# A decoder layer's down projection computed as seven block products instead of eight

## The chip, the cores and the metric

The kernel runs on one core of a Trainium2 chip. The metric is device time in microseconds (us) for one execution. Five engines run their own instruction lists in order and wait for each other by semaphores: TensorE (PE in the rows, its weight loads PEld), VectorE (DVE), ScalarE (ACT), GpSimd (POOL) and SyncE (SP), which here issues every DMA.

## The reference

One layer of a hybrid decoder over 1024 tokens of width 1024, in float32. Attention and a recurrent mixer come first; only the feed-forward block at the end bears on the change:

```python
D_MODEL = SEQ = 1024;  D_FF = 2816
...
xn2 = rms_norm(x, norm2_g)
ffn = (jax.nn.silu(xn2 @ w_gate) * (xn2 @ w_up)) @ w_down
return x + ffn
```

The last product, (1024 x 2816) times (2816 x 1024), is the down projection. Its left factor, silu(gate) times up, is called the hidden activation below.

## The kernel before

**Who sets the order.** The program is written as streams, generators that yield instructions. A planner (`Flow`) holds an estimate of every instruction's time and emits next, from the stream that can go first, so the order on each engine is fixed when the program is built. `Wait` and `Mark` in a stream steer the planner alone; on the chip the engines wait for the data and buffers that an instruction touches. `flow.add(rank, stream)` gives a stream its place among others that are ready together.

**Operands.** PE multiplies in a reduced float32. To keep accuracy each factor is split in two: ACT copies it into a rounded high part (`oph`), another engine subtracts that from the source to get the low part (`opl`), in `split`, called by `operand` (line 1587). A product then takes three matmuls: high times high, high times low, low times high (`passes`). `operand` works on blocks of 128 x 512 and keeps NOPS = 5 pairs of buffers, so operand n can be prepared once operand n - 5 has been read by PE for the last time. Loaded blocks lie in NFRAW = 6 buffers, `fraw`, filled by `fetch_ff` (line 1568) through SP. Every matmul here is 128 x 128 times 128 x 512.

**Gate and up stage.** `ffproj` (line 1659) goes through 22 feature blocks p of 128. From p = NCL = 2 on it already uses a seven-product scheme over the two halves of the tokens and of the width: products P1, P6, P2, P7, P5, P4, P3, twelve matmuls each, 84 for a block p. POOL prepares the low parts of three operands and two weight sums (`sw`), DVE the other sums and low parts. `gates` and `hidden` (lines 1685 and 1712) add the products up from PSUM into `uu` and `up`, apply silu on ACT, multiply, and store the hidden activation, feature by token, to DRAM (`h_d`).

**Down projection.** `down` (line 1762) loops over two token halves th, 22 feature blocks f, two halves of the output columns and four token blocks, with three matmuls each: 2 x 22 x 2 x 4 x 3 = 1056. For a pair (th, f) three operands are loaded and prepared, one of `h_d` and two of `w_down`, all low parts on DVE. Eight PSUM banks accumulate over f. `finals` (line 1787) adds each bank to the residual `acc[j]` and stores it.

Below, a *turn* means the work on one pair of operands in the changed down projection: twelve matmuls.

## Time and profile before

| what | before |
|---|---|
| median of three runs | 1492.36 us (1490.73 to 1492.68) |
| the profiled execution | 1501.24 us, of it span of the trace 1499.4 us |
| granted clock of TensorE over the span, full speed = 1 | 0.973 |
| PE busy over the span | 1426.3 us (95%) |
| DVE / ACT / POOL busy | 801.1 / 714.3 / 539.8 us |
| HBM read / written | 130.26 / 37.75 MB |

How to read it: "busy" is the time in which an engine has an instruction under way. A matmul's row lasts 389 ns because its end is modelled at the end of the pipeline; the next one starts about 0.227 us after it. A "window" row gives the busy time of each engine in a stretch of the span. "Idle before <- releaser" names the instruction that ended the wait.

### The profile page before, as it was taken

To read this page: it belongs to the slowest core of one execution; us is meant where nothing else is said; L and a number is where in the kernel's file an instruction comes from. 1 tells how busy PE (TensorE), PEld (TensorE's weight loads), DVE (VectorE), ACT (ScalarE), POOL (GpSimd) and SP (SyncE) were. 2 spreads that over 40 slices of the span, in tenths; PEclk is the share of its full clock that TensorE was granted. 3 is DMA by queue.
4 is the path that set the end of the run, shared out by engine and by line. 5 is a ranking of instruction groups with operands and counts; after the bars stand their busy time and mean duration, and the time that the engine had idled before them with its cause. 6 is when DMAs were issued, how large, how long until landed. Compare 5 with 4: busy or idle time off the path is not lost. (4 is left out here: it accounts for less than half of the span.)

```text
span 1499.4 us, 24765 instructions
## 1 busy us (share of the span) xinstructions
PE 1426.3 (95%) x8710; PEld 1155.9 (77%) x8710; DVE 801.1 (53%) x1799; ACT 714.3 (48%) x1768; POOL 539.8 (36%) x564
## 2 busy tenths in 40 slices
PE   8999989999999986799999899999999999999999
PEld 5677767777778865688888678888888888888887
DVE  5456677657656337666776734443444434334334
ACT  5434556576676775555855433333333333333332
POOL 4432344255645451422454733444444440000000
PEclk8999999999999988799999999999999999999999
DMA  5343222323323344998521222222222224445443
GB/s 192 108 120 75 65 82 78 99 76 110 115 87 103 105 150 125 276 248 224 151 63 50 84 78 85 85 83 79 75 79 80 85 77 134 148 148 197 148 148 126
DMA packets 199789, 173.83 MB, mean 116 GB/s; under 512 B 39025, under 2 KB 150897, under 8 KB 199666
## 3 DMA queue, kind: packets, MB, share of 16 engines
q1 hardware_dynamic: 199666, 172.26, 38.3%
q8 instruction: 69, 1.13, 0.3%
q14 instruction: 54, 0.44, 0.1%
HBM read 130.26 MB, written 37.75 MB: 112 GB/s over the span
## 5 line engine op out<-in xcount | busy, mean ns | idle before, releaser
L235 ACT ACTIVATE oph<-fraw 128x512 fp32r<-128x512 f32 x208 | 126.3, 627 | 228.7 <-PE chain L235 97.9
L235 POOL TENSOR_TENSOR opl<-fraw,oph 128x512 fp32r<-128x512 f32 x76 | 99.6, 1315 | 220.6 <-PE bank L235 71.3
L235 DVE TENSOR_TENSOR opl<-fraw,oph 128x512 fp32r<-128x512 f32 x132 | 87.5, 689 | 143.6 <-ACT oph L235 143.6
L235 ACT ACTIVATE oph<-sw 128x512 fp32r<-128x512 f32 x80 | 50.6, 632 | 179.4 <-DVE sw L235 71.5
L235 POOL TENSOR_TENSOR inlo<-inraw,inhi 128x512 fp32r<-128x512 f32 x62 | 82.2, 1326 | 84.8 <-ACT inhi L235 70.6
L235 PE MATMUL bank<-opl,oph 128*128 128x512 f32 x176 | 68.5, 389 | 0.0
L235 PE MATMUL bank<-oph 128*128 128x512 f32 x176 | 68.5, 389 | 0.0
L235 PE MATMUL bank<-oph,opl 128*128 128x512 f32 x176 | 68.5, 389 | 0.0
L235 DVE TENSOR_TENSOR opl<-sw,oph 128x512 fp32r<-128x512 f32 x80 | 56.0, 699 | 21.0 <-ACT oph L235 17.2
L235 DVE TENSOR_TENSOR uu<-bank,uu 128x512 f32<-128x512 f32 x20 | 13.8, 692 | 81.7 <-PE bank L235 81.7
L235 DVE SCALAR_TENSOR_TENSOR S<-chain,ec,Sp 64x64 f32<-64x64 f32 x112 | 31.6, 282 | 43.1 <-PE chain L235 38.5
L235 ACT ACTIVATE Ub<-chain 64x64 f32<-64x64 f32 x128 | 28.2, 220 | 54.6 <-DVE VS L235 52.4
L235 POOL TENSOR_TENSOR sw<-fraw 128x512 f32<-128x512 f32 x40 | 52.0, 1299 | 0.0
L235 ACT ACTIVATE Y<-chain 64x64 f32<-64x64 f32 x128 | 26.9, 212 | 51.1 <-DVE S L235 45.8
L235 ACT ACTIVATE inhi<-inraw 128x512 fp32r<-128x512 f32 x62 | 38.7, 624 | 16.7 <-DMA inraw<-in_w_in_dram 6.7
L235 DVE COPY Rb<-chain 64x64 f32<-64x64 f32 x128 | 28.9, 226 | 27.9 <-PE chain L235 25.4
L235 POOL TENSOR_TENSOR up<-up,sg 128x512 f32<-128x512 f32 x20 | 32.3, 1617 | 30.1 <-POOL sw L235 16.1
L235 ACT ACTIVATE sb<-sb,mx 128x256 f32<-128x256 f32 (+3 forms) x64 | 36.2, 567 | 14.4 <-DVE mx L235 14.3
L235 PEld LDWEIGHTS bank<-oph,opl 128*128 128x128 f32 x176 | 33.0, 188 | 6.9
L235 PEld LDWEIGHTS bank<-oph 128*128 128x128 f32 x176 | 33.0, 188 | 6.8
L235 PEld LDWEIGHTS bank<-opl,oph 128*128 128x128 f32 x176 | 33.0, 188 | 6.8
L235 POOL TENSOR_TENSOR rsf<-smf,nhalf 128x8 f32<-128x8 f32 x16 | 26.6, 1662 | 31.6 <-DVE smf L235 31.3
(494 smaller groups left out, 4228.6 us busy)
## 6 DMA issues: line engine op xcount, KB each, us to landing
fraw<-in_w_down_dram SPq DMA_DIRECT2D x88, 256.0 KB, 2.8
inraw<-in_w_in_dram SPq DMA_DIRECT2D x62, 256.0 KB, 2.9
fraw<-in_w_gate_dram SPq DMA_DIRECT2D x48, 256.0 KB, 3.7
fraw<-in_w_up_dram SPq DMA_DIRECT2D x48, 256.0 KB, 3.0
fraw<-h_d SPq DMA_DIRECT2D x44, 256.0 KB, 2.9
h_d<-up SPq DMA_DIRECT2D x42, 256.0 KB, 2.1
rkv_d<-stage SPq DMA_DIRECT2D x24, 256.0 KB, 2.9
xt<-in_x_dram SPq DMA_DIRECT2D x8, 512.0 KB, 7.3
```

The source lines that it names most:

```text
L235: op.fn(*op.a, **op.k)
```

## The change

The eight block products of the down projection become seven over pairs of feature blocks (2m, 2m+1), in Winograd's form of Strassen's scheme. The hidden activation, as A11, A12, A21, A22 by token half and by feature block of the pair, gives four sums S1 to S4; w_down, as B11 to B22 by feature block and by column half, gives four sums T1 to T4. The seven products are P1 = A11 B11, P2 = A12 B21, P3 = S4 B22, P4 = A22 T4, P5 = S1 T1, P6 = S2 T2, P7 = S3 T3, each over m = 0 to 10: 77 turns of twelve matmuls.

- `weight_sums` (new): while the gate and up stage runs, POOL forms T1 to T4 from w_down in the buffers of `acc0` and `acc1`, whose residual is spilled to DRAM and loaded again afterwards; SP stores the sums to `t_d`.
- `halves` (new, in `hidden`): DVE forms S1 to S4 (for a pair of blocks p six operations where there were two); SP stores them to `s_d`. A21 is no longer stored.
- `fetch_ff`: the first three turns are loaded through `fraw`, the others through four new buffers `raw2` in the space of B22, which PE reads up to its last product of the gate and up stage.
- `prepare_ff`: the low part of a turn's first operand (a, of the hidden activation) stays on DVE, that of its second (b, of the weights) goes to POOL.
- `finals`: P1 goes to `acc` and, by ACT, to `U2`; P6 is added to `U2` by DVE, and POOL then adds `U2` to three parts of `acc` for each of four token blocks. P4 accumulates on P7's banks and P3 on P5's once DVE has read them (`dtaken`).

```diff
-    blocks2 = [(th, f, j, "down") for th in range(2) for f in range(NFF) for j in range(3)]
...
+    turns2 = [(x, m) for x in ("P1", "P6", "P7", "P4", "P5", "P3", "P2") for m in range(NP)]
+    factors = {"P1": ("A11", "B11"), "P2": ("A12", "B21"), "P3": ("S4", "B22"), "P4": ("A22", "T4"),
+               "P5": ("S1", "T1"), "P6": ("S2", "T2"), "P7": ("S3", "T3")}
+    NEARLY = NFRAW // 2
...
+        yield Wait(("P3", NFF - 1))
+        for n, (x, m) in enumerate(turns2[NEARLY:]):
+            if n >= 4:
+                yield Wait(("rawfree2", n - 4))
+            raw = T(PX, [128, 2, 4, 128], F32, "raw2", tag="x1", bufs=4)
+            for j in range(2):
+                src, mark = factor(factors[x][j], m)
+                yield Wait(*([mark] if mark else []))
+                yield SP.dma_start(raw[:, j].rearrange("p k t -> p (k t)"), src)
...
+    def weight_sums():
...
+        yield Wait(*[("x2", i) for i in range(4, 8)])
+        for m in range(NP):
+            ws = [T(pacc, [128, 2, HB], F32, f"ws{i}", tag=f"acc{i}") for i in range(2)]
+            for i in range(2):
+                f = 2 * m + i
+                yield SP.dma_start(ws[i].rearrange("p q t -> p (q t)"), w_down[f * 128:(f + 1) * 128, :])
+            (b11, b12), (b21, b22) = [[w[:, q, :] for q in range(2)] for w in ws]
+            for j, o_, a_, b_ in ((1, b11, b12, b11), (3, b12, b22, b12), (2, b22, b22, b11), (4, b21, b21, b22)):
+                yield POOL.tensor_tensor(out=o_, in0=a_, in1=b_, op=ALU.subtract)
+                yield SP.dma_start(t_d[j - 1][m * 128:(m + 1) * 128], o_)
...
+        for n, (x, m) in enumerate(turns2):
+            for j in range(2):
+                key = (x, m, j, "down")
+                yield Wait(("raw", key))
+                yield from operand(key, fraws[key], POOL if j else DVE)
...
+    flow.add(23, weight_sums())
...
+            if p % 2 == 0:
+                held[0] = T(PG, [128, HB], F32, "first", bufs=4)
+                yield DVE.tensor_tensor(out=held[0], in0=c22, in1=c12, op=ALU.mult)
+                held[1] = T(PG, [128, HB], F32, "first", bufs=4)
+                yield DVE.tensor_tensor(out=held[1], in0=c21, in1=held[0], op=ALU.subtract)
+                yield SP.dma_start(s_d[2][both], held[1])
...
+            else:
+                yield DVE.tensor_tensor(out=c22, in0=c22, in1=c12, op=ALU.mult)
+                yield SP.dma_start(h_d[rows, HB:S], c22)
...
+                yield DVE.tensor_tensor(out=s2, in0=c22, in1=held[1], op=ALU.subtract)
+                yield SP.dma_start(s_d[1][both], s2)
...
+    after = {"P4": "P7", "P3": "P5"}
...
+        for x, m in turns2:
...
+            for t in range(4):
+                if m == 0 and x in after:
+                    yield Wait(("dtaken", after[x], t))
+                    downs[x, t] = downs[after[x], t]
...
+                for n, (a_, b_) in enumerate(passes(ah, al, bh, bl)):
+                    yield PE.matmul(out=downs[x, t][0], lhsT=a_[:, t, :], rhs=b_.rearrange("p k t -> p (k t)"),
...
+                if x == "P1":
+                    yield ACT.activation(U2[:, t, :], ps, AF.Copy)
+                yield DVE.tensor_tensor(out=out_, in0=ps, in1=out_, op=ALU.add)
...
+                if x == "P6":
+                    for i, c in ((t, hi), (4 + t, lo), (4 + t, hi)):
+                        yield POOL.tensor_tensor(out=acc[i][:, c], in0=acc[i][:, c], in1=U2[:, t, :], op=ALU.add)
```

The order on PE, DVE, ACT, POOL and SP is the same in both programs up to the feed-forward block. Three places in it, with the rows as the built programs have them (tiles, output before input; the number behind a tile tells buffers apart).

SP in the gate and up stage, before: one block p (`up` holds hidden activations, `fraw` the loaded weights).

```order
L235 DMA fraw<-in_w_up_dram 128x4x128
L235 DMA h_d<-up_11329 128x512
L235 DMA h_d<-up_11310 128x512
L235 DMA fraw<-in_w_up_dram 128x4x128
L235 DMA fraw<-in_w_gate_dram 128x4x128 x2
```

SP at the same place, after (`ws` weight sums, `first` held S sums).

```order
L235 DMA t_d<-ws_10435 128x512
L235 DMA fraw<-in_w_up_dram 128x4x128
L235 DMA t_d<-ws_10435 128x512
L235 DMA h_d<-up_10519 128x512
L235 DMA t_d<-ws_10436 128x512
L235 DMA s_d<-first 128x512
L235 DMA fraw<-in_w_up_dram 128x4x128
L235 DMA fraw<-in_w_gate_dram 128x4x128 x2
L235 DMA t_d<-ws_10436 128x512
L235 DMA ws_10607<-in_w_down_dram 128x1024
L235 DMA ws_10608<-in_w_down_dram 128x1024
```

The stores of weight sums, which wait for POOL, and the stores of S sums, which wait for DVE, now stand ahead of weight loads that were there alone.

POOL in the gate and up stage, before: one block p.

```order
L235 TENSOR_TENSOR up_11776<-up_11776,sg_11717 128x512
L235 TENSOR_TENSOR opl<-fraw,oph 128x512 x2
L235 TENSOR_TENSOR sw_11872<-fraw 128x512
L235 TENSOR_TENSOR opl<-fraw,oph 128x512
L235 TENSOR_TENSOR sw_11912<-fraw 128x512
L235 TENSOR_TENSOR up_11925<-up_11925,sg_11866 128x512
```

POOL at the same place, after.

```order
L235 TENSOR_TENSOR opl<-fraw,oph 128x512
L235 TENSOR_TENSOR sw_10627<-fraw 128x512
L235 TENSOR_TENSOR ws_10607<-ws_10607 128x512
L235 TENSOR_TENSOR opl<-fraw,oph 128x512
L235 TENSOR_TENSOR sw_10670<-fraw 128x512
L235 TENSOR_TENSOR ws_10607<-ws_10608,ws_10607 128x512
L235 TENSOR_TENSOR up_10683<-up_10683,sg_10621 128x512
L235 TENSOR_TENSOR ws_10608<-ws_10608,ws_10607 128x512
L235 TENSOR_TENSOR opl<-fraw,oph 128x512
L235 TENSOR_TENSOR ws_10608<-ws_10608 128x512
```

Four subtractions on `ws` now stand between the low parts, the `sw` sums and the product `up`.

POOL at the end of the gate and up stage, before; it has nothing behind these rows.

```order
L235 TENSOR_TENSOR sw_12806<-fraw 128x512
L235 TENSOR_TENSOR up_12819<-up_12819,sg_12760 128x512
L235 TENSOR_TENSOR opl<-fraw,oph 128x512
L235 TENSOR_TENSOR up_12969<-up_12969,sg_12909 128x512
L1856 UNCONDITIONAL_BRANCH
```

POOL after, where the down projection goes from P6 to P7 (`raw` is raw2, `U` is U2; the first row is the b operand of P7's turn 0).

```order
L235 TENSOR_TENSOR opl<-raw_13658,oph 128x512
L235 TENSOR_TENSOR acc_11600<-acc_11600,U_13477 128x512
L235 TENSOR_TENSOR acc_6839<-acc_6839,U_13477 128x512
L235 TENSOR_TENSOR opl<-raw_13681,oph 128x512
L235 TENSOR_TENSOR acc_6839<-acc_6839,U_13477 128x512
L235 TENSOR_TENSOR opl<-raw_13704,oph 128x512
L235 TENSOR_TENSOR acc_11604<-acc_11604,U_13477 128x512
L235 TENSOR_TENSOR opl<-raw_13727,oph 128x512
L235 TENSOR_TENSOR acc_6840<-acc_6840,U_13477 128x512 x2
L235 TENSOR_TENSOR opl<-raw_13751,oph 128x512
```

The low part of every turn now goes through POOL, and between those of P7's turns 0 to 9 stand twelve additions to `acc`.

## Rows read from the trace of the kernel before

**Rows 1.** The page: span; busy time of each engine, share of span, count
```profile
span 1499.4 us, 24765 instructions
...
PE 1426.3 (95%) x8710; PEld 1155.9 (77%) x8710; DVE 801.1 (53%) x1799; ACT 714.3 (48%) x1768; POOL 539.8 (36%) x564
```

**Rows 2.** Busy by stage: window, length, each engine with count, PEclk, DMA share, GB/s
```profile
1064.94:1084.23 19.29, 19.29 (x86) 15.76 (x85) 7.80 (x13) 6.14 (x10) 8.00 (x6) 1.00 0.27 82
1260.00:1490.00 230.00, 229.99 (x1015) 190.15 (x1014) 88.28 (x135) 75.06 (x126) 0.00 (x0) 1.00 0.44 148
```

**Rows 3.** Timeline, first and last matmul of the down projection, and last sum
```profile
1255.88 0.39 PE L235 MATMUL mm<-oph 128*128 128x512 f32 x1
...
1495.38 0.39 PE L235 MATMUL chain<-oph,opl 128*128 128x512 f32 x1
...
1495.80 0.69 DVE L235 TENSOR_TENSOR acc<-chain,acc 128x512 f32<-128x512 f32 x1
```

**Rows 4.** The page, groups: engine, op, tiles, count; busy us, mean ns; idle
```profile
L235 PE MATMUL bank<-opl,oph 128*128 128x512 f32 x176 | 68.5, 389 | 0.0
...
L235 DVE TENSOR_TENSOR opl<-fraw,oph 128x512 fp32r<-128x512 f32 x132 | 87.5, 689 | 143.6 <-ACT oph L235 143.6
...
L235 POOL TENSOR_TENSOR opl<-fraw,oph 128x512 fp32r<-128x512 f32 x76 | 99.6, 1315 | 220.6 <-PE bank L235 71.3
```

**Rows 5.** Timeline, down projection: end of a reader, then the next operands
```profile
1353.36 0.39 PE L235 MATMUL chain<-opl,oph 128*128 128x512 f32 x1
...
1353.79 1.15 ACT L235 ACTIVATE oph<-fraw 128x512 fp32r<-128x512 f32 x2 [1.86 <-PE chain L235]
...
1354.46 1.29 DVE L235 TENSOR_TENSOR opl<-fraw,oph 128x512 fp32r<-128x512 f32 x2 [1.80 <-ACT oph L235]
```

**Rows 6.** Timeline, gate and up stage: ACT to POOL, and POOL to ACT
```profile
863.47 0.63 ACT L235 ACTIVATE oph<-fraw 128x512 fp32r<-128x512 f32 x1 [0.37 <-PE bank L235]
...
864.18 1.30 POOL L235 TENSOR_TENSOR opl<-fraw,oph 128x512 fp32r<-128x512 f32 x1 [2.53 <-ACT oph L235]
...
1058.99 1.28 POOL L235 TENSOR_TENSOR sw<-fraw 128x512 f32<-128x512 f32 x1
...
1060.30 0.63 ACT L235 ACTIVATE oph<-sw 128x512 fp32r<-128x512 f32 x1 [2.83 <-POOL sw L235]
```

**Rows 7.** Timeline, start of the gate and up stage: DVE beside POOL
```profile
840.54 1.27 POOL L235 TENSOR_TENSOR tt<-tt,B11l 128x512 f32<-128x512 f32 x1 [1.76 <-DVE tt L235]
...
841.05 0.69 DVE L235 TENSOR_TENSOR tt<-bank,B11h 128x512 f32<-128x512 f32 x1
...
846.14 1.73 POOL L235 TENSOR_TENSOR T3l<-t,T3h 128x512 fp32r<-128x512 f32 x1
...
846.66 1.75 DVE L235 TENSOR_TENSOR tt<-tt,B21l 128x512 f32<-128x512 f32 x1
...
848.34 1.77 DVE L235 TENSOR_TENSOR T2l<-tt,T2h 128x512 fp32r<-128x512 f32 x1
```

**Rows 8.** Timeline, gate and up stage: SP load issues, and a load's first reader
```profile
1060.30 0.37 SPq L235 DMA_DIRECT2D fraw<-in_w_up_dram  x1
...
1065.65 0.43 SPq L235 DMA_DIRECT2D fraw<-in_w_up_dram  x1
...
1072.91 1.29 POOL L235 TENSOR_TENSOR sw<-fraw 128x512 f32<-128x512 f32 x1
```

**Rows 9.** The page, DMA issues: median us from issue to landing, last column
```profile
fraw<-in_w_down_dram SPq DMA_DIRECT2D x88, 256.0 KB, 2.8
...
xt<-in_x_dram SPq DMA_DIRECT2D x8, 512.0 KB, 7.3
```

**Rows 10.** Timeline and windows around a wait of PE before the stage
```profile
745.32 0.66 PE L235 MATMUL chain<-kk,qv 128*128 128x128 f32 x4 [1.81 <-ACT qv L235]
...
746.00:748.00 2.00, 2.00 (x15) 2.00 (x15) 1.12 (x5) 2.00 (x7) 2.00 (x2) 0.80 0.06 21
...
748.00:750.00 2.00, 2.00 (x9) 1.81 (x9) 0.55 (x1) 2.00 (x6) 1.78 (x3) 0.50 0.68 181
...
750.00:752.00 2.00, 2.00 (x15) 1.82 (x15) 1.83 (x11) 0.40 (x2) 1.12 (x1) 0.85 0.21 81
```

More of the change, by code (lines that the diff above doesn't have):

```diff
@@ L304, in hymba_kernel @@
     h_d = dram.tile([DFF, S], F32, name="h_d")
+    s_d = [dram.tile([DFF // 2, HB], F32, name=f"s{j}_d") for j in range(1, 5)]
+    t_d = [dram.tile([DFF // 2, HB], F32, name=f"t{j}_d") for j in range(1, 5)]
+    spill_d = dram.tile([2 * 128, D], F32, name="spill_d")
     def pow_rsqrt(o, i):
@@ L1572, in fetch_ff @@
             raw = T(pf, [128, 4, 128], F32, "fraw", bufs=NFRAW)
[L1573 to L1583 removed]
+            p, r, q, kind = key
@@ L1627, in prepare_ff @@
             yield from operand((p, "S4"), s4, DVE)
-        for key in blocks2:
-            yield Wait(("raw", key))
-            yield from operand(key, fraws[key], DVE)
-            yield Mark(("rawfree", key))
+        for n, (x, m) in enumerate(turns2):
[3 more added lines that the diff above has]
+                yield from operand(key, fraws[key], POOL if j else DVE)
+                if n < NEARLY:
+                    yield Mark(("rawfree", key))
+            if n >= NEARLY:
+                yield Mark(("rawfree2", n - NEARLY))
     flow.add(7, load_g2())
@@ L1725, in hidden @@
             yield Free(banks2[p, "f"][1])
-            yield DVE.tensor_tensor(out=c22, in0=c22, in1=c12, op=ALU.mult)
-            yield SP.dma_start(h_d[p * 128:(p + 1) * 128, HB:S], c22)
-            yield Mark(("h", p, 1))
+            yield from halves(p, sg0[p], c22, c12)
         for p in range(NCL, NFF):
@@ L1745, in hidden @@
             yield Wait(("P4", p), ("sg0", p))
-            c21 = T(pf, [128, HB], F32, "up0", tag="g2bc")
+            held[2] = T(pf, [128, 2, HB], F32, "up0", tag="g2bc")
+            c21 = held[2][:, 0, :]
             yield plus(c21, p, "c", u2)
@@ L1755, in hidden @@
             yield ACT.activation(c12, c12, AF.Silu)
[L1756 to L1758 removed]
+            yield from halves(p, c21, c22, c12)
     downs = {}
+    after = {"P4": "P7", "P3": "P5"}
     def down():
         yield Wait(("P3", NFF - 1))
[L1765 to L1785 removed]
@@ L1787, in finals @@
-    def finals():
-        for th in range(2):
-            for hf in range(2):
-                for i in range(4):
-                    j = 4 * th + i
-                    cs_ = slice(hf * HB, (hf + 1) * HB)
-                    yield Wait(("dsum", th, i, hf))
-                    ps, tag = downs[th, i, hf]
-                    yield DVE.tensor_tensor(out=acc[j][:, cs_], in0=ps, in1=acc[j][:, cs_], op=ALU.add)
-                    yield Free(tag)
-                    yield SP.dma_start(out[j * 128:(j + 1) * 128, cs_], acc[j][:, cs_])
+        for x, m in turns2:
+            keys_ = [(x, m, j, "down") for j in range(2)]
+            yield Wait(*[("op", k) for k in keys_])
+            (ah, al, na), (bh, bl, nb) = [fops[k] for k in keys_]
+            for t in range(4):
+                if m == 0 and x in after:
+                    yield Wait(("dtaken", after[x], t))
+                    downs[x, t] = downs[after[x], t]
+                elif m == 0:
+                    tag = yield Get()
+                    downs[x, t] = bank(tag), tag
+                for n, (a_, b_) in enumerate(passes(ah, al, bh, bl)):
+                    yield PE.matmul(out=downs[x, t][0], lhsT=a_[:, t, :], rhs=b_.rearrange("p k t -> p (k t)"),
+                                    start=(m == 0 and n == 0 and x not in after), stop=(m == NP - 1 and n == 2), skip_group_check=True)
+                if m == NP - 1:
+                    yield Mark(("dsum", x, t))
+            for n in (na, nb):
+                yield Mark(("opused", n))
@@ new lines, in finals @@
+    def finals():
+        lo, hi = slice(0, HB), slice(HB, D)
+        U2 = None
+        for x in dict.fromkeys(x for x, m in turns2):
+            second, cols, last = {"P1": (0, lo, False), "P6": (0, hi, False), "P7": (4, hi, False), "P4": (4, lo, True),
+                                  "P5": (4, hi, True), "P3": (0, hi, True), "P2": (0, lo, True)}[x]
+            for t in range(4):
+                yield Wait(("dsum", x, t), "acc")
+                ps, tag = downs[x, t]
+                if U2 is None:
+                    U2 = T(PG, [128, 4, HB], F32, "U2", tag="T1h")
+                out_ = U2[:, t, :] if x == "P6" else acc[second + t][:, cols]
+                if x == "P1":
+                    yield ACT.activation(U2[:, t, :], ps, AF.Copy)
+                yield DVE.tensor_tensor(out=out_, in0=ps, in1=out_, op=ALU.add)
+                if x in after.values():
+                    yield Mark(("dtaken", x, t))
+                else:
+                    yield Free(tag)
+                if x == "P6":
+                    for i, c in ((t, hi), (4 + t, lo), (4 + t, hi)):
+                        yield POOL.tensor_tensor(out=acc[i][:, c], in0=acc[i][:, c], in1=U2[:, t, :], op=ALU.add)
+                if last:
+                    yield SP.dma_start(out[(second + t) * 128:(second + t + 1) * 128, cols], acc[second + t][:, cols])
```

80 lines of the change are left out of this document (43 added, 37 removed).

## The prediction

> **What bounds the kernel now.** I read the page first: PE is busy for 1426.3 of 1499.4 us [rows 1]. Then the windows by stage, since a share over the whole span hides which stage is full. In one block p of the gate and up stage PE is busy for all of its 19.29 us, and in the down projection for 229.99 of 230 us, at a granted clock of 1.00; DVE, ACT and POOL are below half, and POOL does nothing at all in the down projection [rows 2]. So both stages that the change touches are bound by PE, and a matmul that goes away there shortens the span by itself, as long as the others keep up. Last I read the timeline for how an operand gets ready, because the change gives PE two new operands per twelve matmuls where it had three per twenty-four, and gives POOL a place in that chain.
>
> **Removed: 132 matmuls.** The down projection has 1056 matmuls (the loops of `down`); its first starts at 1255.88 and its last at 1495.38 [rows 3], so one takes 239.50 / 1055 = 0.227 us, and twelve 2.724. The 389 ns of a matmul's row [rows 4] overlap with the next. The new stage has 77 turns of twelve, 924 matmuls of the same shape and, as the three-pass loop shows, in the same order on a bank. 132 x 0.227 = 30.0 us less. The programs' order shows all 924, so that the matmuls don't go away is no case. Were they to run at the pace of the gate and up products, 19.29 / 84 = 0.2296 [rows 2], the stage would be 924 x 0.0026 = 2.4 us longer; I take 0.227, since both factors are `oph` and `opl` tiles as before.
>
> **The chain of one turn.** With five buffers, the b operand of a turn can only be made once the turn two before it has let go of a buffer. Let that turn end at 0, so that the next runs from 0 to 2.72 and ours starts there. ACT starts 0.04 after the end of the last matmul that read the buffer (1353.36 + 0.39 = 1353.75, then 1353.79) [rows 5]. That is the last but one of the turn, which starts at -0.45 and ends at -0.06; ACT goes from -0.02 to 0.61 (0.63 each). POOL starts 0.08 behind ACT (863.47 + 0.63 = 864.10, then 864.18) [rows 6], takes 1.30 and ends at 1.99; the engine behind it starts 0.03 later (1058.99 + 1.28 = 1060.27, then 1060.30). PE wants the low part of b for its second matmul, at 2.72 + 0.23 = 2.95. So 0.9 us are left, and the steady turns cost nothing. The a operand has a whole turn more. ACT has 1.26 us of work per turn, DVE 0.69, POOL 1.30, of 2.72. Loads: two of 256 KB per turn, landing after 2.8 us [rows 9], with four turns of raw buffers ahead; nothing waits for them.
>
> **POOL and DVE hold each other up.** At 846 us POOL does an operation in 1.73 us that takes 1.27 elsewhere, and DVE one in 1.75 that takes 0.69, whenever both are at tiles in SBUF [rows 7, 4]; the two alternate. I count 0.46 us of POOL's time for each such DVE operation that falls between POOL's. A DVE operation that reads a PSUM bank does not do this: at 841.05 one takes 0.69 beside POOL's 1.27 [rows 7]. The Trainium skill (GPSIMD Engine Reference, Key points) draws the same line: POOL contends with DVE instructions that have two SBUF inputs. Were the four `U2` additions from PSUM counted as well, the term below would be 4 x 0.46 = 1.8 us larger; by the rule, which the row bears out, they are not.
>
> **Added: twelve POOL additions in P7.** They stand between the low parts of P7's turns 0 to 9, in POOL's fixed order. From the end of the low part for turn 0, at 1.99 - 2.72 = -0.73 before P7 begins, to PE's need of the one for turn 9, at 9 x 2.724 + 0.23 = 24.75, POOL has 25.5 us. It must do nine low parts and twelve additions, 21 x 1.30 = 27.3 us: 1.8 us too late. With one DVE low part (two SBUF inputs) per turn between them, 9 x 0.46 = 4.1 more: 5.9 us. While POOL has no pause DVE always finds it busy, as at 846 us, so I take 5.9; 1.8 stays as the lower end. It falls where POOL has two additions ahead of a low part, at turns 1, 4 and 8, and PE waits there for POOL. Against this stands a rule: the Trainium skill (GPSIMD Engine Reference, Engine selection) would have two-input elementwise work on VectorE, GpSimd being about twice as slow; here it is 1315 against 689 ns [rows 4]. By it, with the b low parts on DVE (1.38 of 2.72 us), this term would be nil and the sum 5.9 us lower.
>
> **Added: sums in the gate and up stage.** Per block p, while the weight sums last (eleven of them, one per p), POOL has three low parts, two `sw`, `up` and four subtractions, 10 x 1.30 = 13.0 us, and nine DVE operations on SBUF (four low parts, two `sw`, one product, on average two of the new S operations) cost it up to 9 x 0.46 = 4.1: 17.1 of 19.29. It fits, though with little left. The five operand buffers let POOL be late by several us before PE notices, since an operand is made some four products ahead. DVE gets 2 x 0.69 = 1.4 us more on top of 7.80 [rows 2]. On SP, the second `up` load of a block, issued at 1065.65 and first read at 1072.91 [rows 8], now stands behind the store of T2 and of an S sum. It has 7.26 us and needs 2.8; at the worst landing of the page, 7.3 for 512 KB loads queued together [rows 9], it would have nothing left. I take 1 us for the whole stage, mostly for its beginning where POOL is already full, between 0 and the price of rival C.
>
> **Added: hand-overs.** The first three turns come through `fraw`, and give 8.2 us to the loads that wait for PE to let go of B22 (2.8 us, then some 2.5 to prepare). P4's first turn needs P7's banks read by DVE: a bank is full one quarter of a turn after another (0.68), DVE reads it in 0.69, and P4 comes to the same bank a whole turn later; no wait. The last sums and stores are those of before: DVE starts 0.03 after PE's end [rows 3]. All of this at zero.
>
> **The sum.** -30.0 + 5.9 + 1.0 = -23.1 us. The profiled execution took 1501.24 us (1499.4 of span and 1.8 around it) and would take 1478.1. The median of the runs shown, 1492.36, lies 8.9 us below that execution; I take the same difference from it: **1469.3 us**.
>
> **The rivals.**
> A. *All hidden.* POOL and DVE interleave without loss and the stage before is covered: -30.0 + 0 to 1.8, 1462.4 to 1464. For it: all averages are low. Against it: the alternation at 846 us [rows 7].
> B. *The b operand late in every turn.* If POOL needs more than 1.30 + 0.9 = 2.2 us per low part, PE waits 77 times; 0.1 us over costs 7.7, 0.3 over 23. Time 1477 to 1492. For it: the buffers allow no work ahead. Against: 1315 ns on average over 76 [rows 4], and even with a DVE meeting 1.76.
> C. *Slower: POOL and DVE fill the gate and up stage.* If each meeting costs the path what DVE loses in one, 1.75 - 0.69 = 1.06, instead of 0.46, a block needs 13.0 + 9 x 1.06 = 22.5 us against 19.29, and eleven blocks lose 3.25 x 11 = 36: 1469 + 36 = 1505. It ends slower than before from 23.1 / 11 = 2.1 us per block on. For it: the order is fixed by a planner that has no price for a meeting. Against it: the 17.1 above, and the buffers.
> D. *The clock falls.* After a wait of 1.81 us the granted clock read 0.80, 0.50 and 0.85 in windows of 2 us [rows 10], below full speed by 2 x (0.20 + 0.50 + 0.15) = 1.7 us of work. Three waits of that size in P7: 5.1 us more, 1474.4. Against it: only 1.3 to 1.7 us each, with PE full between, while PE in [rows 10] was idle before as well. [...]
>
> **How the numbers follow.** My forecast (1466 to 1472) 0.47, A 0.19, D 0.10, B 0.13, C 0.11. The range 1461 to 1484 takes in the forecast, A, D and about half of B: 0.82. A difference of 0.2%, 3 us, is about what a measurement of this kernel can tell. Faster by more than that: forecast, A, D and most of B, 0.86; within it: the end of B and the beginning of C, 0.04; slower: C, 0.10.
>
> **What would show it.** Right: PE's twelve matmuls at 2.72 us in P1 and from P4 on; waits of PE for `opl` from POOL in P7, three of over 1 us, 5 to 6 in sum; blocks p at 19.3 us. Wrong: a block p of 20 us or more (C), a wait for POOL in every turn (B), no wait in P7 (A), a clock below 1.00 there (D). What I fear most is POOL's delays in the gate and up stage reaching SP, whose stores wait for POOL, and through SP the weight loads.

## The result and the profile after

The changed kernel took 1474.12 us, the median of four runs (1470.15 to 1475.64), against 1492.34 for the kernel before on the same chip: 0.9876 of it, with a 95% interval of 0.9854 to 0.9898, or **18.2 us less** (15.2 to 21.8). A second comparison, made with the experiments below, gave 1476.95 against 1490.51, 0.9893 (0.9863 to 0.9922). The forecast was 23.1 us less. So the direction held and the size was some 5 us too large: 1474.12 lies above the forecast of 1466 to 1472 and inside the range of 1461 to 1484. The traces say where the 5 us are.

The page of after, of the lines that answer to [rows 1] and [rows 4] the span, PE, DVE and POOL, and the two groups of low parts:

```profile
span 1473.9 us, 24927 instructions
PE 1394.2 (95%) x8578; PEld 1125.4 (76%) x8578; DVE 898.7 (61%) x1800; ACT 723.8 (49%) x1794; POOL 731.7 (50%) x697
...
L235 DVE TENSOR_TENSOR opl<-raw,oph 128x512 fp32r<-128x512 f32 x74 | 97.1, 1312 | 89.1 <-ACT oph L235 89.0
...
L235 POOL TENSOR_TENSOR opl<-raw,oph 128x512 fp32r<-128x512 f32 x74 | 97.7, 1320 | 91.9 <-ACT oph L235 84.7
```

There are 132 fewer matmuls, as the change says, and POOL now works in the down projection too. The low parts on DVE last 1312 ns on average where they took 689 [rows 4]; those on POOL are as before. The feed-forward block can be cut in two by its first product (`B11h`) and the first and last matmul of the down projection. The rows of after, from PE's timeline (start, duration, what it is; in brackets how long PE was idle before it and for whom):

```profile
802.45 1.10 PE L235 MATMUL bank<-B11h,oph 128*128 128x512 f32 x4
...
1254.71 0.39 PE L235 MATMUL mm<-oph 128*128 128x512 f32 x1
...
1469.64 0.39 PE L235 MATMUL mm<-oph,opl 128*128 128x512 f32 x1
```

The same first product in the kernel before:

```profile
811.33 1.10 PE L235 MATMUL bank<-B11h,oph 128*128 128x512 f32 x4
```

Ahead of this product the code is the same, so the 8.9 us between 811.33 and 802.45 are no part of the change. They belong to that one execution of before, which also lay 8.9 us above its median: in the thirteen other traces of this case the product begins at 799.5 to 804.6.

| stretch | before | after | difference | forecast |
|---|---|---|---|---|
| gate and up, first product to first matmul of the down projection | 444.55 | 452.26 | **+7.7** | +1.0 |
| down projection, first to last matmul ([rows 3] for before) | 239.50 | 214.93 | **-24.6** | -24.1 (-30.0 + 5.9) |
| last matmul to the end of the span | 4.07 | 4.22 | +0.2 | 0 |
| sum | | | -16.7 | -23.1 |

The sum lies within the interval of the runs, and it puts the miss into one stretch. The windows of after show its kind: block 2 (from the first product of that block on), block 5, which like blocks 3 to 10 has weight sums beside it, and P6, P7 and P4 of the down projection. Columns: the window, its length, busy time of PE, PEld, DVE, ACT, POOL with the instructions, the granted clock, the DMA share and GB/s.

```profile
861.60:887.97 26.37, 21.55 (x86) 17.19 (x85) 15.69 (x16) 6.55 (x11) 16.67 (x13) 0.87 0.60 201
926.55:945.84 19.29, 19.29 (x86) 15.76 (x85) 12.71 (x14) 6.02 (x10) 14.82 (x11) 1.00 0.57 192
1284.65:1314.57 29.92, 29.92 (x134) 24.77 (x132) 17.32 (x16) 13.20 (x25) 14.93 (x12) 1.00 0.62 193
1314.57:1350.05 35.48, 32.27 (x133) 24.07 (x132) 13.68 (x16) 12.67 (x23) 32.67 (x23) 1.00 0.51 163
1350.05:1380.04 29.99, 29.99 (x133) 24.76 (x132) 17.20 (x16) 12.69 (x23) 14.22 (x11) 1.00 0.60 197
```

Eleven turns take 29.92 us, 2.72 each, and P7 takes 35.48: 5.6 more, as in the fourth row, where POOL is busy for nearly all of the time. The other six products last 29.9 to 30.0 each. In the gate and up stage every block from block 3 on takes 19.3 us (one takes 19.5). Block 2 alone takes 26.37, where it took 19.90 before (869.40 to 889.30): **6.5 of the 7.7 us are in this one block**.

Some 1.1 us more lies ahead of block 2 (59.15 against 58.07), and that is not the change. Over all fourteen traces this part lasts 57.7 to 58.1 us in nine, the kernel before among them, and 58.8 to 59.6 in five. These five are the ones with one more stretch of 3.4 us at a granted clock of 0.50 there, behind a wait of PE of 2.3 us that all fourteen have: from 828 to 830 us the clock reads 0.65 in the trace of after, and 1.00 in that of the same kernel run once more (below).

### The profile page after: what moved, and what is told of

It is laid out like the page before. It is cut to its first block, busy times and chain, and to the rows that moved or that the text cites. A ratio compares the mean times of both kernels' runs of the same rounds, so it can differ in the third digit from the quotient of the medians.

```text
span 1473.9 us, 24927 instructions
## 1 busy us (share of the span) xinstructions
PE 1394.2 (95%) x8578; PEld 1125.4 (76%) x8578; DVE 898.7 (61%) x1800; ACT 723.8 (49%) x1794; POOL 731.7 (50%) x697
## 5 line engine op out<-in xcount | busy, mean ns | idle before, releaser
L235 POOL TENSOR_TENSOR opl<-fraw,oph 128x512 fp32r<-128x512 f32 x79 | 112.4, 1425 | 152.6 <-ACT oph L235 35.9
L235 DVE TENSOR_TENSOR opl<-raw,oph 128x512 fp32r<-128x512 f32 x74 | 97.1, 1312 | 89.1 <-ACT oph L235 89.0
L235 ACT ACTIVATE oph<-raw 128x512 fp32r<-128x512 f32 x148 | 85.5, 624 | 119.0 <-PE mm L235 66.7
L235 POOL TENSOR_TENSOR opl<-raw,oph 128x512 fp32r<-128x512 f32 x74 | 97.7, 1320 | 91.9 <-ACT oph L235 84.7
L235 DVE TENSOR_TENSOR opl<-sw,oph 128x512 fp32r<-128x512 f32 x80 | 65.5, 819 | 33.5 <-ACT oph L235 33.4
L235 ACT ACTIVATE oph<-fraw 128x512 fp32r<-128x512 f32 x82 | 51.1, 626 | 60.4 <-PE bank L235 20.0
L235 PE MATMUL bank<-opl,oph 128*128 128x512 f32 x154 | 60.0, 390 | 0.0
L235 PE MATMUL bank<-oph 128*128 128x512 f32 x154 | 60.0, 390 | 0.0
L235 ACT ACTIVATE inhi<-inraw 128x512 fp32r<-128x512 f32 x62 | 38.7, 624 | 17.1 <-DMA inraw<-in_w_in_dram 7.1
L235 POOL TENSOR_TENSOR ws<-ws 128x512 f32<-128x512 f32 x22 | 33.2, 1508 | 22.8 <-DMA ws<-in_w_down_dram 19.1
L235 DVE COPY VS<-chain 64x128 f32<-64x128 f32 x64 | 18.9, 295 | 31.9 <-PE chain L235 30.6
```

The source lines that it names most:

```text
L235: op.fn(*op.a, **op.k)
```

## What happens at block 2

The timeline of after from the start of block 2 (P1's first matmuls) to P2, the engines that matter (DVE and POOL at work on SBUF tiles, ACT's two copies, the matmul that waits):

```profile
861.60 1.10 PE L235 MATMUL mm<-B11h,oph 128*128 128x512 f32 x4
...
864.99 1.78 DVE L235 TENSOR_TENSOR up<-up 128x512 f32<-128x512 f32 x1
...
866.80 0.69 DVE L235 TENSOR_TENSOR up<-up,first 128x512 f32<-128x512 f32 x1
867.15 3.13 POOL L235 TENSOR_TENSOR ws<-ws,ws 128x512 f32<-128x512 f32 x2 [0.93 <-DMA ws<-in_w_down_dram]
867.41 1.75 DVE L235 TENSOR_TENSOR first<-up,first 128x512 f32<-128x512 f32 x1
...
869.09 1.75 DVE L235 TENSOR_TENSOR sw<-fraw,sw 128x512 f32<-128x512 f32 x1
...
870.95 0.63 ACT L235 ACTIVATE oph<-sw 128x512 fp32r<-128x512 f32 x1 [6.60 <-DVE sw L235]
871.48 0.58 ACT L235 ACTIVATE first<-mm 128x512 f32<-128x512 f32 x1
872.11 2.07 PE L235 MATMUL mm<-B21h,oph 128*128 128x512 f32 x4 [4.82 <-ACT first L235]
```

The same place in the kernel before:

```profile
869.40 1.10 PE L235 MATMUL mm<-B11h,oph 128*128 128x512 f32 x4
...
870.81 0.68 DVE L235 TENSOR_TENSOR up<-up 128x512 f32<-128x512 f32 x1
...
871.41 0.68 DVE L235 TENSOR_TENSOR sw<-fraw,sw 128x512 f32<-128x512 f32 x1
...
874.28 0.63 ACT L235 ACTIVATE oph<-sw 128x512 fp32r<-128x512 f32 x1 [2.13 <-PE bank L235]
874.82 0.58 ACT L235 ACTIVATE first<-mm 128x512 f32<-128x512 f32 x1
875.45 1.19 PE L235 MATMUL mm<-B21h,oph 128*128 128x512 f32 x4 [0.35 <-ACT first L235]
```

Read it from the bottom. P2 adds onto the bank of P1, so PE may begin it only after ACT has copied P1 out (`first`). In ACT's order that copy stands behind the high part of another operand, `oph<-sw`, for S4, which PE needs only at the end of the block. Before, `sw` was ready at 872.09 and ACT made the operand at 874.28, when PE had let go of a buffer: `sw` had 2.2 us of room. Now `sw` comes 6.55 us later, counted from the start of P1 of block 2 (869.40 before, 861.60 after: 2.69 and 9.24 us to its end). Less the 2.2 us that is 4.4, and the wait grew by 4.5, from 0.35 to 4.82. Four things add up to the 6.55 us: DVE comes to the product `up` 2.0 us later, since POOL, which has weight sums between its `sw` sums, hands it work later; this product is drawn out from 0.68 to 1.78 by a meeting with POOL (1.2 later for what follows); two S sums stand between it and `sw` (2.3); and `sw` is drawn out too (1.1).

Why block 2 alone? From block 3 on, in both kernels and in every block, ACT's order is the other way round: the copy stands ahead of this operand. In block 5 of after:

```profile
929.53 0.60 ACT L235 ACTIVATE first<-bank 128x512 f32<-128x512 f32 x1 [0.25 <-PE bank L235]
...
932.07 1.09 PE L235 MATMUL bank<-B21h,oph 128*128 128x512 f32 x4
...
933.92 0.63 ACT L235 ACTIVATE oph<-sw 128x512 fp32r<-128x512 f32 x1 [3.80 <-DVE sw L235]
```

DVE's `sw` is late here as well, and ACT comes to `oph<-sw` 1.85 us after P2 has begun. PE does not wait for it.

The wait is only a part of the price. Windows of 2 us of after, the granted clock in the third column from the right:

```profile
868.00:870.00 2.00, 0.00 (x0) 0.00 (x0) 2.00 (x2) 0.00 (x0) 1.92 (x2) 0.89 0.52 192
870.00:872.00 2.00, 0.00 (x0) 0.00 (x0) 2.00 (x2) 1.05 (x2) 1.87 (x2) 0.50 0.87 271
872.00:874.00 2.00, 1.89 (x5) 1.50 (x6) 1.71 (x3) 0.06 (x1) 0.00 (x0) 0.50 1.07 318
874.00:876.00 2.00, 2.00 (x6) 1.61 (x5) 0.00 (x0) 0.02 (x1) 0.00 (x0) 0.50 1.05 397
```

The clock falls from 1.00 to 0.50, from 2.4 to 1.2 GHz, while PE is idle, and stays there for the first 4 us of P2: four matmuls take 2.07 us, where they take 1.10 elsewhere. Of the 6.5 us, 4.5 are the longer wait and 2.0 the slow matmuls behind it.

## The experiments on block 2

**The changed kernel once more.** Was the loss at block 2 one of the kernel or of one run?

> The changed kernel once more, on the same chip and against the same runs of the kernel before. The wait before P2 of block 2 was 4.8 to 6.2 us in five kernels in which nothing of the gate and up stage is altered; I expect one in that range again, a gate and up stage of 451 to 454 us, a down projection of 214.9 us, and a time of 1470 to 1476. If the stage is under 447, the loss at block 2 is not one of the kernel but of single runs.

It was there again: a wait of 6.31 us, a gate and up stage of 452.96, a down projection of 214.88, 1476.95 us (above the expected 1470 to 1476 by a little). The stage is 8.4 us longer than before, and all of that is in block 2, which takes 28.46 us. In all six traces in which nothing of the gate and up stage is altered, the wait is 4.8 to 6.3 us and block 2 takes 26.4 to 28.5 us.

**Weight sums later.**

```diff
-        yield Wait(*[("x2", i) for i in range(4, 8)])
+        yield Wait(("h", 3, 1))
         for m in range(NP):
```

> The changed kernel with the weight sums beginning once block 3 is done, and not at the beginning of the gate and up stage. Theory M (POOL full at the beginning of the stage, and DVE's operations drawn out by meetings with it, make `first` of block 2 late): the wait of 4.8 us before P2 of block 2 and the dip of the clock behind it go; the gate and up stage falls from 452.3 us to 445 to 447, the time by 5 to 7 us against the changed kernel, to 1467 to 1469 where the kernel before has 1492. Rival S (the S sums that stand ahead on DVE make it late, whatever POOL does): 450 to 452, time as the changed kernel. Rival L (the lateness comes with the sums wherever they begin): the wait of about 4.8 us comes again at block 4 or 5, 452.

1468.29 us, 0.983 of before (0.9809 to 0.9851); gate and up stage 445.67. PE's row at the same place:

```profile
867.72 1.19 PE L235 MATMUL mm<-B21h,oph 128*128 128x512 f32 x4 [0.70 <-ACT first L235]
```

Theory M held, and rival S is out. No wait comes where the sums now begin, so rival L is out too: from block 3 on the same work is hidden.

**`first` earlier.** POOL and DVE keep their work; one edge of the plan moves. In the changed kernel the mark that releases this copy stands behind three S sums (`halves`), in the kernel before right behind the product of block 1.

```diff
-                yield Wait(("h", max(p - 2, NCL - 1), 1))
+                yield Wait(("c22h", 1) if p == NCL else ("h", max(p - 2, NCL - 1), 1))
...
                 yield DVE.tensor_tensor(out=c22, in0=c22, in1=c12, op=ALU.mult)
+                yield Mark(("c22h", p))
```

> The changed kernel with one edge of the plan moved: ACT's copy `first` of block 2 is released by the product of block 1 and no longer by the three S sums behind it, which puts it one place earlier in ACT's order, ahead of the high part of S4's operand. POOL and DVE have the same work. Theory O (the loss at block 2 is one of order: `first` stood behind an operand that nobody needs yet): the wait of 4.8 us goes, the gate and up stage falls from 452.3 to 446 or 447, the time by 5 to 6 us. Rival: POOL and DVE are late anyway and PE waits for the next operand instead, 4 us or more of wait within blocks 2 and 3; gain below 2 us.

1467.25 us, 0.9831 (0.9815 to 0.9847); gate and up stage 446.36. P2 follows P6 at once, with the clock at 1.00, although DVE's `sw` is as late as it was: it ends 9.25 us after the start of P1 (858.92 to 868.17), against 9.24. The lateness of DVE then meets PE further on, before P3 of block 2, but with 0.81 us only, and block 2 takes 20.4 us. So the rival is out too: one place in ACT's order turned a lateness that costs some 1 us into one that costs 6.5.

**Without the weight subtractions, and without the S sums.** Both leave out work that the output needs, as their expectations say (one run each, 1482.24 and 1470.79 us).

```diff
-                yield POOL.tensor_tensor(out=o_, in0=a_, in1=b_, op=ALU.subtract)
```

> The changed kernel with POOL's 44 subtractions of the weight sums left out (the blocks of w_down are loaded and stored unchanged, so P4, P5, P6 and P7 multiply by the wrong factor); all loads, stores and S sums stay. Theory M (POOL and the meetings with it are what makes block 2 late): the wait before P2 of block 2 falls from 4.8 to below 1 us, gate and up stage 445 to 447 us. Rival S (the S sums ahead on DVE): a wait of 3 us or more stays, 450 or more. Rival D (the traffic of the weight sums, loads that PE's operands wait for): 450 or more, with waits for a load.

```diff
-                yield DVE.tensor_tensor(out=held[1], in0=c21, in1=held[0], op=ALU.subtract)
...
-                yield DVE.tensor_tensor(out=s2, in0=c22, in1=held[1], op=ALU.subtract)
...
-                yield DVE.tensor_tensor(out=held[0], in0=c22, in1=held[0], op=ALU.add)
...
-                yield DVE.tensor_tensor(out=held[1], in0=c21, in1=s2, op=ALU.subtract)
```

> The changed kernel with DVE's S sums (four per pair of feature blocks) left out; the stores stay, with a block of h in the sum's place, so that P3, P5, P6 and P7 multiply by the wrong factor. POOL's weight sums stay. Theory M with two parts: DVE then has two drawn-out operations fewer ahead of `sw` of block 2 (2.3 us by the changed kernel's timeline), so the wait of 4.8 us falls to about 2.4, and the stage to 448 to 449.5. Rival S (the S sums alone are the cause): no wait over 0.7, 445 to 446. Rival P (POOL alone): 4 us or more, 451 to 452.

Without the S sums the wait is 1.40 us, the clock stays at 1.00, and the stage takes 445.50:

```profile
869.28 1.20 PE L235 MATMUL mm<-B21h,oph 128*128 128x512 f32 x4 [1.40 <-ACT first L235]
```

I had expected 2.4 us of wait and 448 to 449.5: the wait fell further, and the clock's share went with it. Without the subtractions the wait at this place is 0.70, as theory M said. Yet the stage grew to 456.68, and the theory's number for it was wrong. New waits of 1.84 and 6.97 us came before P3 of blocks 2 and 3. For the second one, the waits of SP's queue from 885 to 905 us (total, times, longest):

```profile
SPq L235 <- DMA ws<-in_w_down_dram: 8.3, 4, 3.2
```

and the timeline of POOL and PE:

```profile
904.33 1.26 POOL L235 TENSOR_TENSOR sw<-fraw 128x512 f32<-128x512 f32 x1 [8.36 <-DMA fraw<-in_w_up_dram]
...
908.53 2.04 PE L235 MATMUL chain<-B22h,oph 128*128 128x512 f32 x4 [6.97 <-DVE up L235]
```

SP stood for 8.3 us in front of stores of `ws` whose loads had not landed, with the next `up` weights queued behind them; POOL waited for these, DVE for POOL, PE for DVE. That is what rival D of this expectation named, at another place than the wait before P2. In the changed kernel POOL's subtraction lies between load and store, and SP's waits for these loads between 885 and 905 us sum to 1.2 us. So this run answers the question on the wait at block 2; the length of its stage is that of another plan.

Each of the three, POOL's sums, DVE's sums and ACT's order, is enough by its removal to bring the wait from 4.8 or more to 1.4 or less. So a wait of this length needs all three, and none of them makes it alone.

## The experiments on the down projection

**Without the twelve additions.** Part of the output's sum is missing here, as the expectation says.

```diff
-                if x == "P6":
-                    for i, c in ((t, hi), (4 + t, lo), (4 + t, hi)):
-                        yield POOL.tensor_tensor(out=acc[i][:, c], in0=acc[i][:, c], in1=U2[:, t, :], op=ALU.add)
```

> The changed kernel with the twelve POOL additions of U2 into acc left out (so part of the output's sum is missing). My theory: in P7 POOL's order of nine low parts and twelve additions sets PE's pace, and nothing else does; the down projection, from its first matmul to its last, falls from 214.9 us to 923 x 0.227 = 209.5, and no wait of PE for opl is left. Rival: only the three waits that the trace names (3.2 us) are POOL's, and the other 2.2 us come from something else, such as DVE's reads of the banks or the loads; then 211.7.

209.33 us, with no wait in it (1468.45 us in one run). So the additions cost 5.6 us in all, and nothing else slows these 924 matmuls. That answers a puzzle of the changed kernel's trace, where PE's waits in the down projection account for 3.2 us alone (total, times, longest):

```profile
PE mm L235 <- POOL opl L235: 3.2, 3, 1.2
```

The timeline of POOL, PEld and PE at the first turns of P7:

```profile
1313.84 2.99 POOL L235 TENSOR_TENSOR acc<-acc,U 128x512 f32<-128x512 f32 x2
...
1316.78 1.74 POOL L235 TENSOR_TENSOR opl<-raw,oph 128x512 fp32r<-128x512 f32 x1
...
1318.57 0.50 PE L235 MATMUL mm<-opl,oph 128*128 128x512 f32 x1 [0.90 <-POOL opl L235]
1320.24 1.30 POOL L235 TENSOR_TENSOR opl<-raw,oph 128x512 fp32r<-128x512 f32 x1
...
1321.59 0.19 PEld L235 LDWEIGHTS mm<-opl,oph 128*128 128x128 f32 x1 [0.39 <-POOL opl L235]
...
1321.59 0.50 PE L235 MATMUL mm<-opl,oph 128*128 128x512 f32 x1
```

At turns 1, 4 and 8 PE stands idle. At the six other turns up to turn 9 it is late as well, though the profile shows no idle time. The low part of b is what the second matmul streams (`rhs`); the weight load in front of this matmul, of a's high part, waits along with it (0.39 us at 1321.59). It then begins together with the matmul and not beside the one before, the matmul's row lasts 0.50 us where 0.39 is usual, and two matmuls in a row begin 0.31 to 0.35 us apart and not 0.227. That is some 0.2 us each time. Idle time and wider distances together, turns 1 to 9 take 5.6 us longer than nine undisturbed ones.

**The additions on DVE; the b low parts on DVE.**

```diff
-                        yield POOL.tensor_tensor(out=acc[i][:, c], in0=acc[i][:, c], in1=U2[:, t, :], op=ALU.add)
+                        yield DVE.tensor_tensor(out=acc[i][:, c], in0=acc[i][:, c], in1=U2[:, t, :], op=ALU.add)
```

> The changed kernel with the twelve additions in P7 on DVE, where they read two SBUF tiles at 0.69 us, and no longer on POOL. Theory: POOL has then one low part of 1.30 us per turn as everywhere else, the down projection falls from 214.9 to 209.5 to 210.5 us, the time by 4 to 5 us against the changed kernel. Rival: DVE meets POOL at every low part, so that twelve additions and eleven low parts take up to 23 x 1.42 = 33 us of P7's 30 on DVE; PE then waits for the a operand's low part, 212 or more.

```diff
-                yield from operand(key, fraws[key], POOL if j else DVE)
+                yield from operand(key, fraws[key], DVE)
```

> The changed kernel with the low parts of the b operands of the down projection on DVE as well; POOL then has nothing there but the twelve additions in P7. Theory: per turn DVE needs 2 x 0.69 = 1.4 us of 2.72, drawn out only in P7 where it meets the additions (12 x 1.06 = 12.7 us more over 30 us, 22 x 0.69 + 4 x 0.69 + 12.7 = 31 at worst); the down projection falls from 214.9 to 209.5 to 212 us, the time by 3 to 5 us. Rival: in the steady turns both low parts now stand behind each other on DVE, so that the b part comes later than from POOL and PE waits in every turn; over 217 us, slower than the changed kernel. For comparison: the additions on DVE instead of POOL gave 211.1.

The additions on DVE gave 1467.24 us (0.9833, 0.9818 to 0.9849) and a down projection of 211.12; the low parts on DVE 1472.14 (0.9858, 0.9834 to 0.9881) and 212.36. Both gain less in the down projection than was expected (209.5 to 210.5, and at most 212), the first about halfway between its theory's 210.5 and its rival's 212. The times alone would mislead: with the additions on DVE the median is 6.9 us below the changed kernel's 1474.12, of which the down projection gives 3.8, so executions differ by some 3 us elsewhere. PE now waits for DVE, for 0.42 and 0.59 us in the run with the additions on DVE; the second of these waits:

```profile
1327.45 0.50 PE L235 MATMUL mm<-oph,opl 128*128 128x512 f32 x1 [0.59 <-DVE opl L235]
```

The prediction named a rule of the Trainium skill (GPSIMD Engine Reference, Engine selection), by which the b low parts on VectorE would make this term nil. They took 2.6 of the 5.6 us away. Of the other 3.0, 2.4 are in P7, where POOL's additions draw DVE's operations out: in its window DVE (third) is busy for 27.27 of 32.28 us.

```profile
1314.67:1346.95 32.28, 31.18 (x134) 24.39 (x133) 27.27 (x27) 12.68 (x23) 19.65 (x12) 1.00 0.54 180
```

**The slack of a turn.**

```diff
                 yield from operand(key, fraws[key], POOL if j else DVE)
+                if j:
+                    hi, lo, _ = fops[key]
+                    yield POOL.tensor_tensor(out=lo, in0=fraws[key], in1=hi.bitcast(F32), op=ALU.subtract)
```

> The changed kernel with every b low part of the down projection made twice over on POOL (77 operations of 1.30 us more, the same result). It measures the slack of the chain of one turn, which I had worked out as 0.9 us. A b operand is made when the turn two before it ends, so what it is late beyond the slack, 0.4 us and some 0.2 for a weight load that is no longer hidden, is paid once per two turns: 38 x 0.6 = 23 us in the steady turns, and in P7, which POOL paces, 9 x 1.3 = 12 us: the down projection goes from 214.9 to 235 to 250 us. Rival: the slack is over 1.3 us: only P7 grows, 222 to 227. Rival: there is no slack: 1.5 us per two turns, 265 and more.

1520.78 us in one run; the down projection took 257.72, 42.8 more: above the expected 235 to 250 and below the 265 of the third case. P7 is about as reckoned: 46.13 against 35.48, 10.7 more. Every other product of eleven turns takes 34.8 to 37 us where it took 29.9; P6:

```profile
1292.47:1327.35 34.88, 32.82 (x134) 24.00 (x132) 18.35 (x16) 13.66 (x25) 31.71 (x23) 1.00 0.53 166
```

That is 0.9 us per two turns, where I had reckoned 0.6. By the distances between matmuls, one of two turns is late by 0.5 to 0.6 us and the other by 0.1, and in each the uncovered weight load takes 0.1 more. POOL is near its limit as well, busy for 31.71 of 34.88 us with 1.38 per operation. But 22 such operations are 30.4 us, so POOL's pace alone would make a product some 0.4 us longer and not 5.0. The slack is under the 1.3 to 1.4 us of the second operation, since that does cost time. Its size is better read in the changed kernel, a turn of P5 (the first matmul of the turn, ACT's two high parts, POOL's low part):

```profile
1390.89 1.15 ACT L235 ACTIVATE oph<-raw 128x512 fp32r<-128x512 f32 x2 [1.57 <-PE chain L235]
1390.92 0.39 PE L235 MATMUL chain<-oph 128*128 128x512 f32 x1
...
1391.66 1.29 POOL L235 TENSOR_TENSOR opl<-raw,oph 128x512 fp32r<-128x512 f32 x1 [1.43 <-ACT oph L235]
...
1392.08 1.42 DVE L235 TENSOR_TENSOR opl<-raw,oph 128x512 fp32r<-128x512 f32 x1 [1.30 <-ACT oph L235]
```

POOL is done at 1392.95, 2.03 us after the turn's start at 1390.92. PE wants the result 2.95 after it, so 0.92 us are left.

**All of it together.** The two edits on block 2, and the twelve additions spread, four each behind P6, P7 and P4; once on DVE, once on POOL.

```diff
-                if x == "P6":
-                    for i, c in ((t, hi), (4 + t, lo), (4 + t, hi)):
-                        yield POOL.tensor_tensor(out=acc[i][:, c], in0=acc[i][:, c], in1=U2[:, t, :], op=ALU.add)
+                i, c = {"P6": (4 + t, hi), "P7": (4 + t, lo), "P4": (t, hi)}.get(x, (0, None))
+                if c:
+                    yield DVE.tensor_tensor(out=acc[i][:, c], in0=acc[i][:, c], in1=U2[:, t, :], op=ALU.add)
```

> The changed kernel with the late beginning of the weight sums, the early `first` of block 2, and the twelve additions on DVE and spread: four each behind the last product of P6, P7 and P4. The parts add up: gate and up stage 452.3 to 445 or 446, down projection 214.9 to 209.5 to 210.5 (twelve additions at once on DVE gave 211.1), so 10 to 12 us less than the changed kernel, 1462 to 1464 where the kernel before has about 1492. Rival: both halves of the first gain are the same gain and the rest is not spread thin enough: 211 or more for the down projection, 1465 to 1467.

> As the kernel with late sums, early `first` and spread additions, but the additions on POOL as in the changed kernel: the same twelve operations on the same engine, four behind each of three products and not twelve behind one, with mostly one of them ahead of a low part. Theory (what counts is how many additions stand ahead of one low part, and the slack of a turn is some 0.9 us): single additions cost 0.3 us or less each, the two pairs about 1.2 us each; down projection 211 to 213 against 214.9. Rival (twelve times 1.30 us of POOL's time cost the same wherever they stand): 214 to 215.

On DVE 1462.79 us, 0.9812 of before (0.9796 to 0.9828); on POOL 1465.85, 0.9827 (0.9813 to 0.984). Block 2 is back at 19.3 us and the gate and up stage at 443.6 and 443.75, as expected. The down projection was not: 212.41 and 214.40. On DVE, P7 takes 29.92 us, and the loss is new and at one place, P4's first turn. DVE's timeline there, and PE's wait:

```profile
1334.20 1.58 DVE L235 TENSOR_TENSOR acc<-acc,U 128x512 f32<-128x512 f32 x1
1335.70 0.68 DVE L235 TENSOR_TENSOR opl<-raw,oph 128x512 fp32r<-128x512 f32 x1
1336.31 0.68 DVE L235 TENSOR_TENSOR acc<-bank,acc 128x512 f32<-128x512 f32 x1
...
1337.04 0.50 PE L235 MATMUL bank<-oph 128*128 128x512 f32 x1 [1.74 <-DVE acc L235]
```

Between two reads of P7's banks there is now an addition (here a low part as well), and P4 accumulates on these banks. By the distances between matmuls PE loses 3.1 us in this turn. On POOL, the single additions in P7 cost 0.2 us each (30.65 us for P7), and each of the two pairs 1.1 to 1.2, as the theory said. But a hand-over wait of 1.2 us came there too (a drawn-out low part of DVE stands between two bank reads), so the sum was outside of what I expected, and inside the rival's 214 to 215; the parts, not the sum, speak for the theory.

**Reads first.** The four additions behind all four reads:

```diff
-                if x == "P6":
-                    for i, c in ((t, hi), (4 + t, lo), (4 + t, hi)):
-                        yield POOL.tensor_tensor(out=acc[i][:, c], in0=acc[i][:, c], in1=U2[:, t, :], op=ALU.add)
...
+            plus_, c = {"P6": (4, hi), "P7": (4, lo), "P4": (0, hi)}.get(x, (0, None))
+            for t in range(4 if c else 0):
+                yield DVE.tensor_tensor(out=acc[plus_ + t][:, c], in0=acc[plus_ + t][:, c], in1=U2[:, t, :], op=ALU.add)
```

> As the kernel with late sums, early `first` and spread additions on DVE, but with the four additions behind all four reads of a product's banks, and not between them. In the run before, PE waited 2.2 us at the first turn of P4 for DVE, which let go of P7's banks one by one with an addition between two of them. Theory: that wait was all that was left; the down projection falls from 212.4 to 209.5 to 210.3 us, the time to 1459 to 1462. Rival: the four additions in a row then make the low part of an a operand late, a wait of 1 us or more for DVE at each of three places; 211 to 212.5, and the time stays at 1462 to 1464.

**1460.96 us** (1458.19 to 1463.29), 0.979 of before (0.9766 to 0.9814), and below every run of the changed kernel. From P1's first matmul to P2's last it needs 209.30 us with no wait of PE, and the gate and up stage takes 443.57. Block 2 in the window view:

```profile
862.10:881.40 19.30, 19.30 (x85) 15.78 (x84) 10.71 (x15) 5.51 (x9) 8.18 (x6) 1.00 0.35 109
```

## Why the prediction was right, and where it was off

**The 132 matmuls.** Right: 239.50 - 209.30 = 30.2 us in the last kernel, where 30.0 were reckoned. The steady turns take 2.72 us.

**The chain of one turn.** Right, to 0.05 us: the b low part is done 2.03 us after a turn's start (reckoned 1.99), 0.92 us before PE wants it (0.96 by the numbers there). Rival B is out.

**The additions in P7.** Right: 5.6 us against 5.9, with PE's waits at turns 1, 4 and 8. From the end of turn 0's low part (1312.59 + 1.29 = 1313.88) to that of turn 9's (1344.66) POOL took 30.8 us, where 31.4 were reckoned and 25.5 are free; so the 0.46 us per meeting was about the right price. Rival A is out. What was wrong is the sign I gave to look for, three waits of over 1 us and 5 to 6 us in sum: the profile shows 0.90, 1.17 and 1.15, 3.2 in sum, as idle time, and the rest is in the wider distances between matmuls.

**The clock (rival D).** It did not fall in P7: the waits of 0.90, 1.17 and 1.15 us left it at 1.00. It fell at a place that I had not priced, block 2, in a wait of 4.8 us, and cost 2.0 us there. That rival D's time, 1474.4, is nearly the measured one is luck. The Trainium skill (TensorE: Matmul & The Clock Gate, HAM oscillation) tells of a kernel whose matmuls wait for a DMA in every round of a loop, and whose clock falls anew in each of these gaps. By the traces of this case the gap of 4.8 us was one, and those of about 1 us in P7 were not.

**The gate and up stage.** This is the step that failed: a term of 1.0 us "mostly for its beginning where POOL is already full" that measured 7.7, and 8.4 in the second trace. The reason given was that the five operand buffers let POOL be late by several us before PE notices. That holds for operands, and the stage shows it: from block 3 on POOL and DVE carry the same sums at 19.3 us per block. It does not hold for `first`. PE waits for that copy with no buffer between, and in block 2 it stands in ACT's order behind an operand, so that a late operand that nobody needs yet delays it. The rows that said so were there to be read in the kernel before: the wait of 0.35 us at 875.45, and ahead of it `oph<-sw`, whose `sw` had 2.2 us of room. I had counted the work of POOL and not followed what stands behind each of the operations that come late. The count was off too: in the seven blocks from 3 to 9 POOL is busy for 13.3 to 14.9 us, where I had up to 17.1, and DVE for 11.8 to 14.7, where I had 9.2. There it is mostly DVE that pays for the meetings.

**Rival C** named the right ingredients, DVE drawn out from 0.69 to 1.75 by meetings with POOL, and an order without a price for them. But its price was eleven blocks of 3.25 us; it was paid once, because only in block 2 does ACT's copy stand behind the operand that comes late. Of what I feared most, POOL's delays reaching PE through SP and the weight loads, the changed kernel shows no wait of PE; only the kernel without subtractions does.

**Hand-overs.** Right for the changed kernel: P4 takes 29.99 us, the tail 0.2 more. The cover is thin, though: with an addition between two reads of the banks the same hand-over cost 3.1 us.

The wait at block 2 is 4.8 us in one execution and 6.3 in the next, with the same order on every engine. Most of that is PE coming earlier to a copy that is as late as before: counted from the first product of the stage, P2 of block 2 begins after 69.66 and 69.93 us, but P1 after 59.15 and 57.93, since in the first the clock was lower for 3.4 us on the way. What stays open is why the beginning of P2 itself moves between 69.0 and 70.7 us over the six traces of this order.

## What to carry to other kernels

Work that is added to a helper engine is to be followed along every chain in which that engine stands, and not only along the one that has buffers: look for the operation that the bound engine waits for directly (here a copy out of a bank), and at what stands ahead of it in its own engine's order. A small wait at such a place in the profile of before marks the chain; how much lateness it takes is read one step further back, from when that operation's own input was ready (here 2.2 us earlier). Where the order of the two can be turned, as from block 3 on, the lateness costs nothing. And what the profile calls idle is a lower bound for a late operand: count the distance from matmul to matmul, too.

## What the runs showed of the hardware

- When POOL and DVE meet in SBUF, who pays depends on the place: in the steady turns, where DVE begins 0.42 us behind POOL, DVE alone is drawn out (1.42 us at 1392.08, against the 0.69 of [rows 4]) and POOL not at all (1.29); at full load in P7 POOL's operations take 1.3 or some 1.74, and most of DVE's low parts 0.9.
- A matmul that had to wait for an operand costs PE 0.1 to 0.2 us on top of any idle time, since its weight load (0.19 us) waits with it and is then no longer hidden: one or two distances of 0.31 to 0.35 us between matmuls where 0.227 is usual.
- Waits of 0.7 to 1.74 us with PE busy on both sides (block 2 with late weight sums or without S sums, P7, the hand-over to P4) left the granted clock at 1.00; those of 4.8 to 6.3 us at block 2 brought it to 0.50, and the matmuls behind them ran at that level for 3 to 6 us. A wait of 2.3 us ahead of block 2, at the same place in all fourteen traces, was followed by 0.50 in five of them and left 1.00 in nine.
